# Two chained transformer models on one core: eighteen expert weight tiles instead of sixteen, and another join between the models

## The chip, the cores and the metric

The kernel runs on one core of a Trainium2 chip. Its time is the device time of one execution in microseconds (us). Three executions gave 896.29, 896.9 and 897.87 us, a median of 896.9. Profiles are of single executions.

A core has the engines PE (TensorE, matrix products), DVE (VectorE), ACT (ScalarE) and POOL (GpSimd), each with its own instruction stream, and SP (SyncE), which here issues nearly all loads. They wait for each other by semaphores.

## The reference

Two models run one behind the other on the same 256 tokens of width 1024, all in float32. The first has a latent attention with a convolution branch and then a mixture of 32 experts. The change touches the experts, the norm between the models, and the start of the second.

```python
# first_block, its end: one layer (DEPTH = 1), 256 tokens of width 1024
h = rmsnorm(x, norm2_g[l]) * (1.0 + sc2) + sh2
x = x + gt2 * hierarchical_moe(h, ...)
...
return rmsnorm(x, final_norm_g)

def hierarchical_moe(h, rg_w, rg_b, re_w, re_b, e_gate, e_up, e_down):
    t = h.reshape(-1, D)
    g_prob = jax.nn.softmax((t @ rg_w + rg_b).astype(jnp.float32), axis=-1)
    g_val, g_idx = lax.top_k(g_prob, 1)                     # 1 of 4 groups
    ...
    e_val, e_idx = lax.top_k(jax.nn.softmax(e_sel, axis=-1), TOP_K_IN_GROUP)   # 2 of its 8 experts
    ...
    for gi in range(N_GROUPS):
        a = jnp.einsum('td,edf->tef', t, e_gate[gi])        # f = 128
        u = jnp.einsum('td,edf->tef', t, e_up[gi])
        hid = jax.nn.silu(a) * u * combine[:, gi, :, None]
        out = out + jnp.einsum('tef,efd->td', hid, e_down[gi])
    return out.reshape(B, S, D)

# second_block, layer 0: a gated delta mixer, layer 1: an attention with forget gates
mod = cond @ ada_w[i] + ada_b[i]
shift, scale, gate = jnp.split(mod[:, None, :], 3, axis=-1)
h = rmsnorm_2(x, norm_w[i]) * (1 + scale) + shift
x = x + gate * mixer(h, ...)
```

The norm at the end of the first model and the first norm of the second follow on each other directly.

## The kernel before

**Order of work.** `block1_rest` does attention, convolution and output projection of the first model (to about 280 us). `moe` and `moe_loop` route the tokens and run the experts (to about 402 us). `join` adds the experts' output to the residual and does both norms at once, and `gdn` (to about 716 us) and `fox` are the two layers of the second model. A matrix product in near full precision is split in a high and a low part, and its weights pass from `raw` tiles (as loaded) to `hl` tiles (split). An object `feed` puts weight jobs (load, split, products) between other work.

**Experts.** Each token goes to two of 32 experts, and each expert takes up to 32 tokens into its slots; tokens beyond that go to an overflow tile. The experts are worked off in quads of four: eight quads, and the overflow tile as the fifth of nine rounds. For a round i, `s1` is the products with gate and up weights (`ffn1`, L1321), `turn` a transpose (L1333), `s2` the products with the down weights (`ffn2`, L1347), whose result is scaled by `gt2` (`eys`, L1352) and split in `eyh` and `eyl`, and `s3` adds the rows back to the tokens in PSUM (`ffn3`, L1365 and L1366). `pair` gathers the tokens of two quads by a product with a one-hot matrix `hot` (L1401).

**Weights.** The weights of a quad are six tiles of 1 MB (128 x 2048 floats): four with gate and up of one expert, two with the downs of two experts each, 48 tiles in all. A tile lies in a slot of a list `ECYC`, which is gone through in turn: slots of their own (`ex`), of a small ring (`r`), and `raw` and `hl` slots that the first model no longer needs. Sixteen are asked for before the experts start. From then on `weights(i + 1)` asks for the next quad in round i, so that SP issues a load when the slot's last reader is done. SP issues in order: what stands behind a waiting load waits too. In round 2 SP, like every engine, reads the number of overflow tiles (`tot`), and in round 4 all pass a branch (`spill`, L1832) around further overflow tiles, which is not taken with this data: one tile is enough.

**Counts.** The rank of a token in its expert comes from small products in a PSUM tile (`rk`); the count of each expert (`cnt_`, L1678 and L1679) is written to the same tile, behind a copy by DVE (`rks`, L1676). On PE the order is ranks, counts, gather of the first pair.

**Join.** For each half of the columns and each half of the tokens, x + experts is formed by DVE (L1862), multiplied by the norm weight `gfin` (`xg`, by POOL L1864 and DVE L1867), and both are squared and summed (ACT L1858, for one piece DVE `jx`). Small DVE operations and a power on POOL (L1884) give one factor per token; the rows are scaled (`xn`, ACT L1888, DVE L1889), and PE turns them by 16 transposes with the identity (L684). `feat` then applies the modulation of the second model and splits for the first products (L483). The final norm weight lies in a tile `gfin` of a pool that is made when the experts have ended. `A(4)` and `A(5)` are products that make modulation rows of the second model from `adaA` and `adaX` weights (`ada_mul`, L530).

## Time and profile before

| | |
|---|---|
| median of three executions | 896.9 us |
| the profiled execution | 898.32 us |
| its span, first to last instruction | 896.5 us |
| mean granted clock of TensorE | 0.951 |
| PE busy | 789.2 us (88%) |
| DVE busy | 582.7 us (65%) |
| ACT busy | 395.5 us (44%) |
| POOL busy | 287.4 us (32%) |
| moved by DMA | 190.23 MB, mean 212 GB/s |

The busy shares are means over stages that differ: a stage in which PE waits for loaded weights and one in which PE sets the pace stand in the same sum. The granted clock is given as a share of 2.4 GHz, 0.50 being 1.2 GHz. 1.8 us lie between the span and the time of the profiled execution.

### The profile page before, as it was taken

The numbers are of one execution on the slowest core, as the hardware profiler recorded it, in microseconds if no ns is written. First come the engines' busy times: TensorE is split into PE (matmuls) and PEld (weight loads), VectorE is DVE, ScalarE is ACT, GpSimd is POOL, SyncE is SP. The second block draws the span as 40 slices with busy tenths as digits, with TensorE's granted clock in tenths as the row PEclk, the third lists the DMA queues.
The fourth block names the chain that finished last, engine by engine and source line by source line (L and its number), as shares of the span: only waits on it lengthen the run. The fifth ranks groups of instructions, "written<-read, shape, count | busy, mean of one in ns | idle before, by whom it ended". The sixth has DMA issues, their size and how long they took to land.

```text
span 896.5 us, 16456 instructions
## 1 busy us (share of the span) xinstructions
PE 789.2 (88%) x6567; PEld 684.4 (76%) x6567; DVE 582.7 (65%) x1168; ACT 395.5 (44%) x734; POOL 287.4 (32%) x219
## 2 busy tenths in 40 slices
PE   4889798889996998975999799998999998999986
PEld 1578677678885854534789787888998977999976
DVE  1587875755756754336768989568656458667555
ACT  2355433436444222116575244345543462555452
POOL 0144221213323200004273255133354434445433
PEclk9999999999997899996999899899999999999999
DMA  8886667678989599959354267362247654444201
GB/s 286 282 255 208 201 202 253 226 255 302 369 345 345 215 409 372 409 213 334 113 172 144 92 203 269 96 205 81 92 157 268 216 167 138 136 148 142 95 24 48
DMA packets 125813, 190.23 MB, mean 212 GB/s; under 512 B 11243, under 2 KB 84185, under 8 KB 125733
## 3 DMA queue, kind: packets, MB, share of 16 engines
q1 hardware_dynamic: 123252, 185.78, 60.0%
q10 hardware_dynamic: 1984, 1.79, 0.6%
q0 software_dynamic: 496, 1.59, 0.5%
q8 instruction: 52, 0.85, 0.4%
q14 instruction: 29, 0.23, 0.1%
HBM read 187.91 MB, written 1.22 MB: 211 GB/s over the span
## 4 chain that ended last, share of the span: by engine, by line
PE 31%; DVE 13%; POOL 2%; ACT 2%; issue 2%; DMA 0%; POOLq 0%; ACTq 0%; DVEq 0%
PE mm L351 4%; PE mm L352 4%; PE mm L353 4%; DVE cacc L2023 2%; PE mm L483 2%; PE mm L485 2%; PE mm L484 2%; PE tp L2430 1%; DVE zb L2396 1%; PE tp L2437 1%; DVE NU L2229 1%; PE tp L2038 1%; PE mm L391 1%; PE mm L393 1%; PE mm L392 1%
## 5 line engine op out<-in xcount | busy, mean ns | idle before, releaser
L313 POOL TENSOR_TENSOR hl<-raw,hl 128x1024 fp32r<-128x1024 f32 (+3 forms) x82 | 192.5, 2349 | 327.1 <-ACT hl L309 298.7
L309 ACT ACTIVATE hl<-raw 128x1024 fp32r<-128x1024 f32 (+4 forms) x156 | 153.8, 1018 | 45.1 <-DMA raw<-in_w_in_dram 27.7
L313 DVE TENSOR_TENSOR hl<-raw,hl 128x1024 fp32r<-128x1024 f32 (+2 forms) x74 | 98.6, 1333 | 69.5 <-ACT hl L309 69.4
L483 PE MATMUL mm<-h_hi,hl 128*128 128x256 f32 x448 | 135.6, 303 | 3.2 <-DVE b L589 2.5
L485 PE MATMUL mm<-h_hi,hl 128*128 128x256 f32 x448 | 129.9, 290 | 7.0 <-POOL hl L313 3.5
L484 PE MATMUL mm<-h_lo,hl 128*128 128x256 f32 x448 | 129.3, 289 | 0.7 <-DVE h_lo L699 0.7
L483 PEld LDWEIGHTS mm<-h_hi,hl 128*128 128x128 f32 x448 | 88.0, 196 | 10.0 <-ACT hl L309 4.0
L485 PEld LDWEIGHTS mm<-h_hi,hl 128*128 128x128 f32 x448 | 87.8, 196 | 8.8 <-POOL hl L313 4.8
L484 PEld LDWEIGHTS mm<-h_lo,hl 128*128 128x128 f32 x448 | 88.1, 197 | 1.0 <-DVE h_lo L699 1.0
L351 PE MATMUL mm<-hl,h4h 128*128 128x256 f32 (+1 forms) x256 | 75.9, 296 | 1.1 <-ACT h4h L696 0.7
L352 PE MATMUL mm<-hl,h4h 128*128 128x256 f32 (+1 forms) x256 | 72.2, 282 | 0.9 <-DVE hl L313 0.5
L353 PE MATMUL mm<-hl,h4l 128*128 128x256 f32 (+1 forms) x256 | 72.4, 283 | 0.4 <-DVE h4l L699 0.2
L1046 DVE SCALAR_TENSOR_TENSOR tp<-uq,convw,tp 128x256 f32<-128x256 f32 x120 | 58.4, 487 | 3.1
L351 PEld LDWEIGHTS mm<-hl,h4h 128*128 128x128 f32 x256 | 48.8, 190 | 2.7 <-ACT h4h L696 0.9
L352 PEld LDWEIGHTS mm<-hl,h4h 128*128 128x128 f32 x256 | 48.7, 190 | 1.3 <-DVE hl L313 0.7
L353 PEld LDWEIGHTS mm<-hl,h4l 128*128 128x128 f32 x256 | 48.5, 190 | 1.0 <-DVE h4l L699 1.0
L1321 PE MATMUL tp<-ew,xs 128*32 128x256 f32 x528 | 42.7, 401 | 6.4 <-DMA ew<-in_expert_w_up_dram 6.4
L2023 DVE SCALAR_TENSOR_TENSOR cacc<-mm,aconv,cacc 128x255 f32<-128x255 f32 (+2 forms) x96 | 38.8, 472 | 13.6 <-ACT cacc L2020 13.6
L1321 PEld LDWEIGHTS tp<-ew,xs 128*32 128x32 f32 x528 | 26.7, 115 | 23.4 <-issue 14.6
L351 PE MATMUL mm<-hl,h_hi 128*128 128x256 f32 x128 | 38.4, 300 | 0.0
L352 PE MATMUL mm<-hl,h_hi 128*128 128x256 f32 x128 | 36.4, 284 | 0.0
L353 PE MATMUL mm<-hl,h_lo 128*128 128x256 f32 x128 | 36.2, 282 | 0.0
(684 smaller groups left out, 2007.0 us busy)
## 6 DMA issues: line engine op xcount, KB each, us to landing
raw<-in_ada_w_dram SPq DMA_DIRECT2D x30, 1024.0 KB
raw<-in_a_w_in_dram SPq DMA_DIRECT2D x24, 1024.0 KB
ew<-in_expert_w_gate_dram SPq DMA_DIRECT2D x32, 512.0 KB
ew<-in_expert_w_up_dram SPq DMA_DIRECT2D x32, 512.0 KB
ew<-in_expert_w_down_dram SPq DMA_DIRECT2D x16, 1024.0 KB
raw<-in_b_w_in_dram SPq DMA_DIRECT2D x15, 1024.0 KB
raw<-in_w_in_dram SPq DMA_DIRECT2D x12, 1024.0 KB
raw<-in_a_w_out_dram SPq DMA_DIRECT2D x8, 1024.0 KB
```

The costliest lines, as they stand in the source:

```text
L309: nc.scalar.activation(pc[2][:, ks], v[:, ks], AF.Copy)
L313: eng.tensor_tensor(pc[3][:, ks], v[:, ks], pc[2][:, ks].bitcast(F), OP.subtract)
L351: nc.tensor.matmul(pts[t], a, whi[:, k, :], start=kk == 0, stop=False)
L352: nc.tensor.matmul(pts[t], a, wlo[:, k, :], start=False, stop=False)
L353: nc.tensor.matmul(pts[t], b, whi[:, k, :], start=False, stop=kk == ko - 1)
L391: nc.tensor.matmul(pts[t], a, whi[:, k, :], start=kk == 0, stop=False)
L483: nc.tensor.matmul(p[:, b, :], wa, hh[:, kk, :], start=kk == 0, stop=False)
L484: nc.tensor.matmul(p[:, b, :], wa, hl[:, kk, :], start=False, stop=False)
L485: nc.tensor.matmul(p[:, b, :], wb, hh[:, kk, :], start=False, stop=kk == ko - 1)
L1046: nc.vector.scalar_tensor_tensor(dst, u[:, b, tp:tp + 256], w(b, tp), dst, op0=OP.mult, op1=OP.add)
L1321: nc.tensor.matmul(pg[32 * s:32 * s + 32, :], xs[:, k, c0 + 32 * s:c0 + 32 * s + 32], gu[s][:, :, k * 128:(k + 1) * 128], start=k == 0, st ...
L2023: nc.vector.scalar_tensor_tensor(acc[:, b, sh:], p[:, b, 0:256 - sh], w(b, 3 - sh), acc[:, b, sh:], op0=OP.mult, op1=OP.add)
```

## The change

It has five parts.

1. `ECYC` has eighteen slots: `r4` and `ex4` are new. Expert 0's gate and up go to `r4` already in `block1_rest`, in front of a load of `in_w_in` weights; the other seventeen are asked for in the order `EFIRST`.
2. `ahead` asks for quads 3 to 7 at fixed places: quad 3 after `s2(0)`, quads 4 and 5 in rounds 2 and 3, quads 6 and 7 after rounds 4 and 5. The downs of the last quad are loaded by halves of the columns, all four experts in one tile, so that each half of `ffn2` needs one tile.
3. The counts are emitted with the ranks, ahead of all DVE reads of that tile.
4. In the join, `gfin` lies in slot `r4`. DVE does all adds and multiplies, ACT all eight squares (scaled by 1/32 before the square, so that the sums are means). Instead of scaling the rows and transposing them, PE multiplies by a diagonal `dg` that holds the factors. `mid` puts the `adaA` products, until now later among the `feed` jobs, between the experts and that.
5. Some buffers share tags (`eys` with `part`, `ptj` with `rowp`, `pw`, `pwt`, `PTx`, `xsx`), the buffers of the overflow tile are taken later, and the scratch for GpSimd's DMAs is 4096 bytes.

```diff
-    ECYC = ["ex2", "ex3", "ex1", "r0", "r1", "raw", "ex0", "raw", "raw", "raw", "hl", "hl", "hl", "hl", "r2", "r3"]
+    ECYC = ["r4", "r0", "r1", "raw", "raw", "raw", "raw", "hl", "ex2", "ex3", "ex4", "ex0",
+            "ex1", "hl", "hl", "hl", "r2", "r3"]
+    EFIRST = [8, 9, 10, 1, 2, 11, 12, 3, 4, 5, 6, 7, 13, 14, 15, 16, 17]
...
+        self.e0 = self.ring(4, "ew", F, 2, 1024)
+        for i, n in enumerate(("gate", "up")):
+            nc.sync.dma_start(self.e0[:, i, :], inp["expert_w_" + n].rearrange("l g e (p j) f -> (l g e) p (j f)", j=8)[0])
...
+                elif q == 7:
+                    nc.sync.dma_start(by_columns(e), down[28:32, :, 512 * (s - 4):512 * (s - 4) + 512]
+                                      .rearrange("e f d -> f e d"))
...
+                for t in range(2):
+                    nc.tensor.matmul(cnt_, self.onesb, mm[:, t], start=t == 0, stop=t == 1)
                 self.picks(hot, iom, rk, 0)
...
                 nc.vector.tensor_copy(rks, rk)
                 rk = rks
-                nc.tensor.matmul(cnt_, self.onesb, mm[:, 0], start=True, stop=False)
-                nc.tensor.matmul(cnt_, self.onesb, mm[:, 1], start=False, stop=True)
...
             if 0 < i < 8:
                 weights(i + 1)
+            if i in (2, 3):
+                ahead(i + 2)
...
             s2(i)
+
+            if i in (0, 4, 5):
+                ahead({0: 3, 4: 6, 5: 7}[i])
...
+                nc.vector.tensor_add(x[:, t, sl], acc[t][n], x[:, t, sl])
+                nc.vector.tensor_mul(xg[:, t, sl], x[:, t, sl], gf[:, sl])
+                for a, o in enumerate((x, xg)):
+                    nc.scalar.activation(junk[:, a, sl], o[:, t, sl], AF.Square, scale=D ** -0.5,
+                                         accum_out=ss[:, a, n, t:t + 1])
+        mid()
...
+        dg = U("dg", "dg", 2, 128)
+        for t in range(2):
+            nc.vector.tensor_scalar(dg[:, t], self.ident, r[:, 1, t:t + 1], None, op0=OP.mult)
...
-        xn = U("xn", "P1", 2, 1024)
         for n in range(2):
             sl = slice(512 * n, 512 * n + 512)
-            nc.scalar.activation(xn[:, 0, sl], xg[:, 0, sl], AF.Copy, scale=r[:, 1, 0:1])
-            nc.vector.tensor_scalar(xn[:, 1, sl], xg[:, 1, sl], r[:, 1, 1:2], None, op0=OP.mult)
...
+                if dg is None:
+                    self.nc.tensor.transpose(o, src, self.ident)
+                else:
+                    self.nc.tensor.matmul(o, src, dg[:, t], start=True, stop=True)
...
-        gf = U("gfin", "MM", 2048)
+        gf = self.ring(4, "gfin", F, 2048)
...
-        feed.add(gq[0], A(4, "A0", "A1"), gq[1], A(5, "X0", "X1"), *gq[2:])
+        fill = A(4, "A0", "A1")
+        feed.add(gq[0])
+        fill.todo = fill.load()
+        feed.add(gq[1], A(5, "X0", "X1"), *gq[2:])
+        def mid():
+            feed.q.insert(0, fill)
+            feed.finish(fill)
```

On SP around the branch (`spill`; in the rows L1832 before, L1859 after), before the change: quad 4's last up and its downs, the branch, then the first loads of quad 5.

```order
L1517 DMA ew<-in_expert_w_up_dram 128x1024
L1520 DMA ew<-in_expert_w_down_dram 128x2x1024 x2
L1832 COMPARE_AND_BRANCH x15
L1832 UNCONDITIONAL_BRANCH x16
L1516 DMA ew<-in_expert_w_gate_dram 128x1024
```

The same place after the change, quad 4's downs, the whole of quad 5, the branch, and the first load of quad 6.

```order
L1535 DMA ew<-in_expert_w_down_dram 128x2x1024 x2
L1528 DMA ew<-in_expert_w_gate_dram 128x1024
L1529 DMA ew<-in_expert_w_up_dram 128x1024
L1528 DMA ew<-in_expert_w_gate_dram 128x1024
L1529 DMA ew<-in_expert_w_up_dram 128x1024
L1528 DMA ew<-in_expert_w_gate_dram 128x1024
L1529 DMA ew<-in_expert_w_up_dram 128x1024
L1528 DMA ew<-in_expert_w_gate_dram 128x1024
L1529 DMA ew<-in_expert_w_up_dram 128x1024
L1535 DMA ew<-in_expert_w_down_dram 128x2x1024 x2
L1859 COMPARE_AND_BRANCH x15
```

Quad 5's ten loads moved ahead of the branch.

On PE at the join, before: the last rows of `ffn3`, then the transposes and the first products of the second model.

```order
L1365 MATMUL tp<-eyh,PTs 128x512
L1366 MATMUL tp<-eyl,PTs 128x512
L684 MATMUL tp<-ident,xn 128x128 x16
L483 MATMUL mm<-h_hi,hl 128x256
L484 MATMUL mm<-h_lo,hl 128x256
```

After the change (one row of the program is one matmul; a plain float32 one leaves two records in a trace):

```order
L1376 MATMUL tp<-eyh,PTs 128x512
L1377 MATMUL tp<-eyl,PTs 128x512
L530 MATMUL tp<-adaA_5870,crep_153 32x512 x4
L530 MATMUL tp<-adaA_5871,crep_153 32x512 x4
L689 MATMUL tp<-dg,xg 128x128 x16
L483 MATMUL mm<-h_hi,hl 128x256
```

The `adaA` products moved in front of the turns, and the turns are products with `dg`.

On DVE at the join, before, from the last `eys` on:

```order
L1352 TENSOR_TENSOR eys<-tp,gt2r 128x512
L1862 TENSOR_TENSOR x<-mm,x 128x512 x2
L1354 TENSOR_TENSOR eyl<-eys,eyh 128x512
L1862 TENSOR_TENSOR x<-tp,x 128x512 x2
L1867 TENSOR_TENSOR xg<-x,gfin 128x512 x2
L1873 TENSOR_TENSOR jx<-x 128x512
L1874 TENSOR_REDUCE jss<-jx 128x1
```

After, from the same `eys` to the diagonal:

```order
L1363 TENSOR_TENSOR eys<-tp,gt2r 128x512
L1886 TENSOR_TENSOR x<-mm,x 128x512
L1365 TENSOR_TENSOR eyl<-eys,eyh 128x512
L1887 TENSOR_TENSOR xg<-x,gfin 128x512
L1886 TENSOR_TENSOR x<-mm,x 128x512
L1887 TENSOR_TENSOR xg<-x,gfin 128x512
L1886 TENSOR_TENSOR x<-tp,x 128x512
L1887 TENSOR_TENSOR xg<-x,gfin 128x512
L1886 TENSOR_TENSOR x<-tp,x 128x512
L1887 TENSOR_TENSOR xg<-x,gfin 128x512
L1895 SCALAR_TENSOR_TENSOR jr<-jss 128x2
```

One add stands before the last `eyl` instead of two, and the multiplies stand directly behind their adds.

## Rows read from the trace of the kernel before

**Rows 1.** windows, the experts at full flow (five engines busy, PEclk, DMA share, GB/s)

```profile
314.00:336.00 22.00, 21.64 (x218) 12.03 (x217) 11.28 (x24) 4.80 (x10) 0.00 (x0) 1.00 1.03 409
```

**Rows 2.** windows, columns as in rows 1, seven stretches

```profile
128.00:132.00 4.00, 4.00 (x31) 3.15 (x33) 1.19 (x2) 2.28 (x3) 0.00 (x0) 1.00 0.95 345
340.00:344.00 4.00, 2.67 (x23) 2.47 (x21) 2.68 (x5) 2.12 (x4) 0.00 (x0) 1.00 0.91 344
344.00:348.00 4.00, 3.34 (x42) 1.57 (x43) 1.42 (x3) 0.63 (x1) 0.00 (x0) 1.00 0.86 292
348.00:352.00 4.00, 4.00 (x42) 2.31 (x34) 1.93 (x4) 0.91 (x2) 0.00 (x0) 1.00 0.96 372
392.00:396.00 4.00, 4.00 (x24) 2.10 (x25) 0.64 (x3) 0.28 (x1) 0.00 (x0) 1.00 0.08 26
404.00:426.00 22.00, 11.51 (x68) 11.22 (x68) 15.67 (x22) 14.42 (x27) 9.53 (x6) 0.61 0.97 335
412.00:416.00 4.00, 2.17 (x10) 2.18 (x11) 2.36 (x6) 3.26 (x6) 2.27 (x3) 0.50 1.09 359
```

**Rows 3.** waits of SP, 230 to 412 us (us, times, longest)

```profile
SPq L2112 <- DVE eyl L1354: 18.8, 1, 18.8
SPq L1520 <- PE tp L1321: 14.0, 1, 14.0
SPq L1516 <- PEq L1832: 9.1, 1, 9.1
```

**Rows 4.** waits of PE, 285 to 416 us

```profile
PE tp L1321 <- DMA ew<-in_expert_w_up_dram: 6.4, 4, 2.0
```

**Rows 5.** timeline (start, length), DVE and PE around the counts

```profile
287.98 2.48 DVE L1647 SCALAR_TENSOR_TENSOR xnl<-xs,rstd,xnh 128x1024 fp32r<-128x1024 f32 x2
...
291.99 0.19 PE L1678 MATMUL tp<-mm,onesb 128*128 128x32 bf16 x1 [4.65 <-DVE rks L1676]
...
298.04 7.40 PE L1321 MATMUL tp<-ew,xs 128*32 128x256 f32 x128
```

**Rows 6.** timeline, the join

```profile
400.04 0.68 DVE L1354 TENSOR_TENSOR eyl<-eys,eyh 128x512 fp32r<-128x512 f32 x1
...
401.31 1.29 DVE L1862 TENSOR_TENSOR x<-tp,x 128x512 f32<-128x512 f32 x2 [0.59 <-PE tp L1366]
401.35 0.39 PE L1366 MATMUL tp<-eyl,PTs 128*128 128x512 f32 x1
...
405.81 2.36 DVE L1867 TENSOR_TENSOR xg<-x,gfin 128x512 f32<-128x512 f32 x2 [3.21 <-DMA gfin<-in_final_norm_g_dram]
...
410.69 0.63 ACT L1858 ACTIVATE gfin<-xg 128x512 bf16<-128x512 f32 x1
411.23 0.19 ACT L1858 ACTIVATION_READ_ACCUMULATOR gfin<-xg 128x1 f32 x1
...
412.28 0.73 POOL L1884 TENSOR_TENSOR jr<-jr,pexp 128x2 f32<-128x2 f32 x1 [3.00 <-DVE jr L1883]
...
413.83 3.67 PE L684 MATMUL tp<-ident,xn 128*128 128x128 f32 x16 [12.09 <-ACT xn L1888]
```

**Rows 7.** timeline, PE, the first half of the last quad

```profile
383.34 8.71 PE L1321 MATMUL tp<-ew,xs 128*32 128x256 f32 x62 [2.01 <-DMA ew<-in_expert_w_up_dram]
```

**Rows 8.** PE groups by shape, 426 to 716 us (busy, mean ns | idle before)

```profile
L2430 PE MATMUL tp<-wk,At 128*128 128x128 f32 x64 | 8.4, 275 | 0.0
...
L2038 PE MATMUL tp<-ident,G 128*128 128x128 f32 x32 | 4.6, 276 | 1.0 <-DVE G L2167 1.0
...
L530 PE MATMUL tp<-adaA,crep 128*32 128x512 f32 x16 | 3.4, 990 | 0.0
...
L530 PE MATMUL tp<-adaX,crep 128*32 128x512 f32 x16 | 1.9, 598 | 0.0
```

**Rows 9.** timeline, SP and ACT where expert 0's tile is to be loaded

```profile
124.94 10.16 SPq L520 DMA_DIRECT2D raw<-in_ada_w_dram  x2
...
129.72 1.06 ACT L309 ACTIVATE hl<-raw 128x1024 fp32r<-128x1024 f32 x1 [2.83 <-DMA raw<-in_w_in_dram]
```

More of the change, by code (lines that the diff above doesn't have):

```diff
@@ L1350, in ffn2 @@
             yl = self.sm.tile([128, 512], R, name="eyl", tag="hft", bufs=2)
-            ys = pool.tile([128, 512], F, name="eys", bufs=1)[:M]
+            ys = self.sm.tile([128, 512], F, name="eys", tag="part", bufs=1)[:M]
             nc.vector.tensor_mul(ys, py[:M], self.gt2[:M, sl])
@@ L1392, in slot_side @@
             nc.tensor.transpose(p[:m, t * 128:(t + 1) * 128], pw[:, t, c0:c0 + m], self.ident)
-        jk = pool.tile([128, 256], B16, name="ptj", bufs=1)
+        jk = self.sm.tile([128, 256], B16, name="ptj", tag="rowp", bufs=1)
         nc.scalar.activation(jk[:m], p[:m], AF.Copy, accum_out=wslot[:m])
@@ L1547, in moe @@
                 own("eyh", 512, dt=R, bufs=2)
-                own("eys", 512)
+                own("xs8", 8, 32)
+                OH = T("OH", 2, 2, 32)
+                T("e2", 2, 32)
                 for t in ("ex0", "ex1", "ex2", "ex3"):
@@ L1837, in tiles @@
                 wsx = pool.tile([128, 1], F, name="wsx", bufs=1)
[L1838 to L1839 removed]
+                PTx = self.const.tile([128, 256], R, name="PTx", tag="crep1", bufs=1)
+                xsx = pool.tile([128, 8, 32], F, name="xsx", tag="xs8", bufs=1)
                 self.slot_side(pool, pwx, 0, 32, PTx, wsx)
@@ L1866, in join @@
-        for t, sl, n in order[2:]:
-            nc.vector.tensor_mul(xg[:, t, sl], x[:, t, sl], gf[:, sl])
-        for a, i in ((1, 0), (0, 2), (1, 1), (1, 2), (1, 3)):
-            square(a, *order[i])
-        t, sl, n = order[3]
-        sq = self.sm.tile([128, 512], F, name="jx", tag="hft", bufs=2)
-        nc.vector.tensor_mul(sq, x[:, t, sl], x[:, t, sl])
-        nc.vector.reduce_sum(ss[:, 0, t, n:n + 1], sq, axis=AX.X)
-        todo = self.feed.q[0].todo
-        todo.pop(0)()
-        sq = self.sm.tile([128, 2, 2], F, name="jsq", bufs=1)
@@ new lines, in join @@
+        mid()
+        todo = self.feed.q[0].todo
+        r = self.sm.tile([128, 2, 2], F, name="jr", bufs=1)
+        nc.vector.scalar_tensor_tensor(r[:, 0], ss[:, 0, 0], EPS, ss[:, 0, 1], op0=OP.add, op1=OP.add)
+        nc.vector.scalar_tensor_tensor(r[:, 1], r[:, 0], EPS, ss[:, 1, 0], op0=OP.mult, op1=OP.add)
+        nc.vector.tensor_add(r[:, 1], r[:, 1], ss[:, 1, 1])
+        nc.gpsimd.tensor_tensor(r[:, 1], r[:, 1], self.pexp.to_broadcast([128, 2]), OP.pow)
+        dg = U("dg", "dg", 2, 128)
@@ L2730, in build @@
             acc = kern.moe(x)
-        if stop == "1":
-            with tc.tile_pool(name="pj", bufs=1) as pool:
-                kern.join(lambda n, tag, *sh, dt=F: pool.tile([128] + list(sh), dt, name=n, tag=tag, bufs=1), acc, x)
         if stop not in ("1a", "1"):
```

90 lines of the change are left out of this document (39 added, 51 removed).

## The prediction

> **What bounds the kernel now.** I read the page's busy shares first (the table above): TensorE (PE) is busy 88% of the span, so time is to be had where PE stands idle or runs at half clock. The windows name the place: the experts and the join behind them, 290 to 415 us. Three views of that stretch carry the argument.
>
> The windows show the weight stream. At full flow the queues move 409 GB/s [rows 1]. The stream has a dent at the spill branch (344, 292, 372 GB/s in three windows from 340 us) and has ended when 392 us are reached (26 GB/s) [rows 2]. SP, which issues all loads in order, waited 14.0 us for the first expert matmuls to give back a slot, 9.1 us for PE's sequencer at the branch, and 18.8 us for the last `eyl` of the experts before it could load the join's norm weight [rows 3]. Meanwhile the consumer waits for bytes: 6.4 us in four waits of `ffn1` for up weights [rows 4]. So from 304 to 392 us the stream is the bound and PE is close behind it; what counts is when the stream restarts and how much is still to come.
>
> The PE rows before that show the second place: 4.65 us idle in front of the counts, because their PSUM tile is first read by DVE (`rks`) [rows 5]. The third is the join: the last expert matmul starts at 401.35 us, the first transpose at 413.83 after 12.09 us of idle PE; in that gap DVE waited 3.21 us for the norm weight, then came squares, a power, a scaling pass, transposes [rows 6].
>
> **Counts.** PE order stays; only the wait goes. The gather could start behind `hot`, but it reads `xnl` too, two DVE instructions that end at 287.98 + 2.48 = 290.46 us [rows 5]. Start 290.5 at once, against 292.1 now (behind the two counts at 291.99): at least -1.6; the whole idle stretch, -4.65, is the other bound, less the run at half clock. The xs copies that follow had waited for `obase`, a DVE chain behind the counts, and the first of those waits goes too. I take -2.8 for the start of `s1(0)` (298.04 now), bounds -1.6 and -3.8. Nothing is behind it on PE that could lose.
>
> **Tiles and `ahead`.** Before, 16 of 48 tiles are loaded when the experts start; after, 18 (one of them, expert 0's, at 124 us). A tile is 1.05 MB, so two fewer are 2.1 MB / 0.409 = 5.1 us of stream. The restart hangs on `s1(0)`, so it moves by its -2.8. Quad 5 is asked before the branch: the dent is (65 + 117 + 37) GB/s x 4 us = 0.88 MB, 2.1 us. The last downs by column halves let the first half of `ffn2` go with one tile, but their pieces are half as long; the nearest row, 335 GB/s in 404 to 426 us where loads of such pieces run [rows 2], gives 2.1 / 0.335 - 5.1 = 1.1 us, of which half lies ahead of the first half. Against it stands one tile fewer to wait for, of which PE could use less than 1 us. I put the pair at 0. Sum for the landing: -5.1 - 2.8 - 2.1 = -10.0.
>
> PE has to follow. Without its waits it gains 6.4 + 2.8 = 9.2, and the last quad's `ffn1`, which took 8.71 us for 62 records against 7.40 for 128 in the first two [rows 5, 7], gives another 1 to 2. So PE could end 10 to 11 us sooner, just enough: both bounds meet, and the last expert matmul moves by **-10.0** (bounds -7, if a slot's reader or the half clock holds one of them, and -11). PE's own wait at the branch, for DVE's sequencer, stays.
>
> **Join.** `gfin` now loads behind the last downs, so DVE's 3.21 us go. DVE then runs add and multiply in turn; POOL's multiplies, `jx` and its reduce are gone. The last `eyl` stands behind one add (0.64), not two: its `eyh` is there half an add earlier, so **-0.3**. From the end E of the last expert matmul: `eyl` ended 1.0 us before E (400.72 to 401.74); behind it stand a multiply, an add, a multiply, to E + 0.95, then the four of the second half, 0.65 each (from the pair of adds of 1.29 us), to E + 3.6. The last square and its read (0.63, 0.19) end at E + 4.5; ACT's eight squares in a row, each behind its DVE row, end there too. Three small DVE instructions follow (four stand now between 411.42 and 412.28, 0.22 each): E + 5.2. The power, 0.73: E + 5.9; two diagonals of 128 columns, the first matmul at E + 6.4 [rows 6]. So 12.09 becomes 6.4: **-5.7**, bounds -4 (DVE multiplies as slow as the pair of 2.36 us now) and -6.5.
>
> **The turning matmuls.** A transpose by `ident` and a plain f32 matmul by `dg` are not the same. In the trace the plain ones leave two records each: 64 records of 128x128 (32 matmuls) take 8.4 us, 0.26 us per matmul; 32 transposes take 4.6 us, 0.14 each [rows 8]. Here the clock is 0.50 [rows 2] and 16 transposes took 3.67 us, 0.23 each [rows 6]. Sixteen matmuls thus take 4.2 us at full clock, 7.4 to 7.7 at half. PE's first GEMM comes right behind, so the loss is on the path: +4 if the clock stays low as long as now, less as PE does more work in that stretch and the clock may rise sooner, and -0.9 at full clock with the GEMM behind it at full clock too. I take **+1.5**, bounds -0.9 and +4.
>
> The Trainium skill, TensorE: Matmul & The Clock Gate, section Terms, calls transpose mode four times as fast for FP32. By the rows here it is 1.8 times. By the page's factor the sixteen would cost 11 us more at half clock instead of 4.
>
> **adaA moved.** Its 16 records cost 3.4 us in a stretch that PE bounds, at half clock by their 990 ns against 598 of `adaX`, whose 16 take 1.9 [rows 8]. They now stand between the experts and the turns. Its loads stand behind `gfin` (0.5 MB) and one `raw` (1 MB), 3.7 MB with its own 2: at 335 GB/s these land 11 us after the last downs, at 392 - 10 + 11 = 393. E moves from 401.35 + 0.39 to 391.4 and the turns from 413.83 to 397.8, so 3.4 us from 393 on fit in the gap with some 1.4 us to spare. Its `part` copy on ACT stands behind the squares. Gain: **-2.4**, bounds -1.9 (the half clock then hits the GEMM) and -3.4. If the landing is 3 us late the cover is gone and each further us counts in full.
>
> **e0.** 1 MB more in front of `raw<-in_w_in` at 124 us: 2.6 us at 0.409, plus two issues of half a microsecond on SP. ACT waits 2.83 us for that load at 129.72 [rows 9]; it will wait longer. PE was busy throughout, all of 128 to 132 us among it [rows 2], and SP itself stood 10 us in the next issue [rows 9], so the stream has slack right behind. **+0.5**, bounds 0 and +3.5.
>
> The renamed buffers and the smaller scratch cost nothing: `eys` and `ptj` share tags with tiles that are idle during the experts; if `part` were needed there, one ACT copy would wait less than 1 us.
>
> **Sum:** -10.0 - 0.3 - 5.7 + 1.5 - 2.4 + 0.5 = -16.4. The profiled execution took 898.32 us, so 881.9; it is 1.4 above the median 896.9, which becomes **880.5**.
>
> **Rivals.**
>
> *PE or DVE takes over as the bound in the experts* (chance 0.15). With the waits gone PE has little left; if the restart gains nothing because `s1(0)` runs at half clock, or a DVE chain (overflow lists before `ehid`) holds the first turn, the last matmul moves by 7 and the half clock in the turns costs 4: 885 to 886. For it: clock 0.50 around the join and PE busy nearly all of 314 to 336 us [rows 1, 2]. Against: each of the four PE waits names the DMA [rows 4].
>
> *The stream stays where it is* (0.10): the change does not do what it says; tiles 18 on wait for slots, or the rate is 380 instead of 409 (30 tiles, 31.5 MB: +6 us). Then only the dent, the join and `adaA` are left: -10.0 + 6 and the rest -6.4, 886.5.
>
> *All covers hold and the clock rises early* (0.12): -11 - 0.3 - 6.5 - 0.9 - 3.4, 875.
>
> *Transposes four times cheaper than matmuls* (0.03): +11 instead of +1.5 gives 890. The records speak against it. It is the mechanism of the page named above.
>
> *Slower: the overflow tile lands late* (0.03). Its buffers are now taken after quad 3 and cleared only when `ffn2(0)` has read one of them; its gathers then share the queues with quads 3 and 4. `s1(8)` needs it at about 330 us. It is issued near 307; if it landed after 330, each us would hold PE, and PE is what everything waits for. From 16.4 us late on, 347 us, the kernel is slower than before. Against: a tile and a half is 4 us of stream, and the slack is over 20.
>
> **How the numbers follow.** My case, -13 to -20, has 0.56: 877 to 884. Range 872 to 888: it takes in the good case, the first two rivals and the bounds of turns and e0, and leaves out 0.15. A measurement tells 0.2%, 1.8 us, from no change. Faster: all but the last case and a remainder in which several bounds fall together, 0.95; same 0.02; slower 0.03.
>
> **What the profile after would show.** PE's wait for `rks` gone and the gather at 290 to 291; `s1(0)` near 295; no dent at the branch; last up weight landing near 380; the four DMA waits of `ffn1` below 3 us in sum; last expert matmul near 391; no wait for `gfin`; first matmul by `dg` at 397 with 32 records in 4 to 7.7 us; `adaA` before it; the first GEMM at 402 to 404. It would be wrong if the matmuls by `dg` hold PE past 405, if `adaA` starts after 394, or if PE in the experts shows new waits for DVE.

## The result, and the profile after

The changed kernel took 881.39 us (median of four executions, 880.5 to 885.71), the kernel before 896.6 us on the same chip. The means, over six executions of the changed kernel and four of the kernel before, have a ratio of 0.9847, interval 0.9815 to 0.9879, so 13.7 us less (10.8 to 16.6); the medians differ by 15.2 us. 880.5 us was forecast, with a range of 872 to 888. Single executions of one kernel differ by up to 11 us here and their granted clocks by about 0.02, so steps of 2 or 3 us are read from stages, not from totals. The execution in the trace after is the slowest of the four, 885.71 us:

```profile
span 883.8 us, 16485 instructions
...
PE 781.9 (88%) x6583; PEld 677.2 (77%) x6583; DVE 580.1 (66%) x1167; ACT 394.7 (45%) x734; POOL 284.1 (32%) x217
```

The share of PE is what it was, so the page does not tell where the time went. Stages do. The table is worked out from starts of PE rows in the timelines: the start of the output projection of the first model (L351, L353), the first `ffn1`, the end of the last `ffn3`, the first turn or transpose at the join, the first small product of the second model (`wba`, L2134 before, L2154 after), the first transpose of `G`, the last PE row. "After again" is a second trace of the same kernel.

| us | to projection | to first `ffn1` | experts | gap at the join | turns to `wba` | `wba` to `G` | rest |
|---|---|---|---|---|---|---|---|
| before | 247.2 | 50.8 | 103.7 | 12.1 | 11.9 | 18.3 | 445.5 |
| after | 249.4 | 46.6 | 96.8 | 5.8 | 10.4 | 18.2 | 449.5 |
| after again | 250.1 | 45.3 | 95.2 | 5.8 | 10.4 | 17.6 | 449.4 |
| forecast, after less before | +0.5 | -2.8 | -7.2 | -6.0 | +1.5 | -2.4 | 0 |
| after less before | +2.2 | -4.2 | -6.9 | -6.3 | -1.5 | -0.1 | +4.0 |
| after again less before | +2.9 | -5.5 | -8.5 | -6.3 | -1.5 | -0.7 | +3.9 |

The rest holds no edit. It took 444.1 to 449.5 us over all kernels below, which have the same code there, and the granted clock in it goes the other way: 0.98 where it took 444.1 us (quad5_late), 0.97 in before, 0.96 in both traces of after. So its +4 goes with the clock and is not bound to the code; why both traces of this kernel lie at the long end is not known.

**Counts** (timeline after, PE and DVE; compare [rows 5]):

```profile
287.96 0.19 PE L1663 MATMUL tp<-mm,n 128*128 128x32 bf16 x1
...
288.10 0.20 PE L1668 MATMUL tp<-mm,onesb 128*128 128x32 bf16 x2
288.94 2.47 DVE L1671 SCALAR_TENSOR_TENSOR xnl<-xs,rstd,xnh 128x1024 fp32r<-128x1024 f32 x2
...
289.18 1.19 PE L1412 MATMUL tp<-hot,xnh 128*128 128x256 f32 x8 [0.87 <-ACT part L533]
...
291.47 1.86 PE L1412 MATMUL tp<-hot,xnl 128*128 128x256 f32 x7 [0.81 <-DVE xnl L1671]
...
295.98 7.28 PE L1332 MATMUL tp<-ew,xs 128*32 128x256 f32 x128
```

The first row of the ranks in the kernel before:

```profile
287.02 0.21 PE L1641 MATMUL tp<-mm,n 128*128 128x32 bf16 x1
```

The counts have no wait in front of them. The gather starts on `xnh` 1.2 us behind the first rank (5.1 before), of which 0.87 are a wait for ACT's `part`, and waits 0.81 us more in its middle, for the `xnl` named in the forecast. From the first rank to the first `ffn1` it is 8.0 us here and 6.7 in the second trace, against 11.0 before, so the counts are worth 3.0 and 4.3 us. The other 1.2 us of that stage's gain lie ahead of the ranks (39.8 us from the projection before, 38.6 in both traces after), where the counts have no part.

**Experts** (three windows after, columns as in [rows 1]; then waits of SP, 230 to 400 us, and of PE, 280 to 410 us: us in all, times, longest):

```profile
340.00:344.00 4.00, 2.06 (x13) 1.32 (x13) 2.14 (x4) 1.13 (x2) 0.00 (x0) 1.00 1.03 410
344.00:348.00 4.00, 4.00 (x66) 2.12 (x65) 2.08 (x4) 1.26 (x2) 0.00 (x0) 1.00 1.02 400
348.00:352.00 4.00, 4.00 (x27) 1.96 (x26) 1.63 (x4) 0.28 (x1) 0.00 (x0) 1.00 1.03 410
```

```profile
SPq L1528 <- PE tp L1332: 11.6, 2, 11.4
```

```profile
PE tp L1332 <- DMA ew<-in_expert_w_up_dram: 4.5, 2, 2.5
...
PE tp L689 <- DVE dg L1901: 1.9, 1, 1.9
...
PE tp L1344 <- DVE ehid L1337: 1.0, 1, 1.0
```

The dent at the branch (344, 292, 372 GB/s in [rows 2]) is gone, and so are SP's waits of 9.1 and 18.8 us in [rows 3]. SP still waits 11.4 us for the first products to give back a slot, and PE still waits for bytes, 4.5 us instead of 6.4 in [rows 4]: the stream is still the bound. The forecast had asked for less than 3 us of such waits.

**Join** (timeline after; compare [rows 6]):

```profile
392.38 0.40 PE L1377 MATMUL tp<-eyl,PTs 128*128 128x512 f32 x1
...
393.00 1.06 PE L530 MATMUL tp<-adaA,crep 128*32 128x512 f32 x8 [0.22 <-DMA adaA<-in_ada_w_dram]
...
395.63 1.07 PE L530 MATMUL tp<-adaA,crep 128*32 128x512 f32 x8 [1.56 <-DMA adaA<-in_ada_w_dram]
...
397.44 0.73 POOL L1898 TENSOR_TENSOR jr<-jr,pexp 128x2 f32<-128x2 f32 x1 [85.89 <-DVE jr L1897]
...
398.20 0.48 DVE L1901 TENSOR_SCALAR dg<-ident,jr 128x128 f32<-128x128 f32 x2 [0.85 <-POOL jr L1898]
...
398.55 3.84 PE L689 MATMUL tp<-dg,xg 128*128 128x128 f32 x32 [1.85 <-DVE dg L1901]
...
402.14 0.36 PE L483 MATMUL mm<-h_hi,hl 128*128 128x256 f32 x1
```

No DVE row waits for `gfin`. The `adaA` products lie in the gap, the second half 1.56 us late but still 1.85 us ahead of the turns; the power comes 5.1 us after the last expert product starts (10.9 before).

**The start** (after, timeline of ACT and a window):

```profile
132.58 1.06 ACT L309 ACTIVATE hl<-raw 128x1024 fp32r<-128x1024 f32 x1 [6.83 <-DMA raw<-in_w_in_dram]
```

```profile
132.00:136.00 4.00, 0.80 (x8) 0.42 (x4) 2.27 (x4) 2.96 (x4) 0.80 (x1) 1.00 0.40 145
```

And the waits of PE, 120 to 160 us:

```profile
PE mm L483 <- DVE gt L589: 2.2, 1, 2.2
PE tp L1276 <- ACT pp L1279: 2.0, 1, 2.0
```

Here something was lost. ACT's wait of 2.83 us in [rows 9] became 6.83, `pp` stands behind it on ACT and PE waits for that; PE was busy 0.80 of four microseconds.

**Behind the join** (timeline after):

```profile
416.82 2.38 POOL L313 TENSOR_TENSOR hl<-raw,hl 128x1024 fp32r<-128x1024 f32 x1 [6.09 <-ACT hl L309]
416.84 2.40 DVE L1926 TENSOR_SCALAR sp<-sp 128x32 f32<-128x32 f32 x1
...
422.65 0.61 PE L2184 MATMUL tp<-g,trile 128*128 128x32 f32 x2 [2.51 <-DVE beta L2170]
...
423.61 3.64 PE L530 MATMUL tp<-adaX,crep 128*32 128x512 f32 x16
```

Where `adaA` had stood, PE now waits 2.51 us for `beta`, and then runs the `adaX` products, which took 1.9 us in [rows 8], at half clock (0.50 granted): 3.64 us.

### The profile page after: what moved, and what is told of

It reads as the page before. It is cut to its first block, busy times and chain, and to the rows that moved or that the text cites. A ratio compares the mean times of both kernels' runs of the same rounds, so it can differ in the third digit from the quotient of the medians.

```text
span 883.8 us, 16485 instructions
## 1 busy us (share of the span) xinstructions
PE 781.9 (88%) x6583; PEld 677.2 (77%) x6583; DVE 580.1 (66%) x1167; ACT 394.7 (45%) x734; POOL 284.1 (32%) x217
## 4 chain that ended last, share of the span: by engine, by line
PE 45%; DVE 24%; DMA 15%; ACT 6%; issue 5%; POOL 3%; SPq 1%; ACTq 0%; POOLq 0%; DVEq 0%
DMA ew<-in_expert_w_up_dram 6%; DMA raw<-in_w_in_dram 6%; PE mm L351 4%; PE mm L353 4%; PE mm L352 4%; PE mm L483 3%; DVE hl L313 3%; PE mm L485 3%; PE mm L484 3%; DVE cacc L2035 2%; DVE tp L1050 2%; POOL hl L313 2%; PE mm L530 2%; ACT hl L309 2%; DMA ew<-in_expert_w_down_dram 1%
## 5 line engine op out<-in xcount | busy, mean ns | idle before, releaser
L483 PE MATMUL mm<-h_hi,hl 128*128 128x256 f32 x448 | 134.4, 300 | 5.5 <-DVE b L589 2.5
L483 PEld LDWEIGHTS mm<-h_hi,hl 128*128 128x128 f32 x448 | 87.5, 195 | 10.9 <-ACT hl L309 4.1
L351 PE MATMUL mm<-hl,h4h 128*128 128x256 f32 (+1 forms) x256 | 76.3, 298 | 1.1 <-ACT h4h L700 0.7
L353 PE MATMUL mm<-hl,h4l 128*128 128x256 f32 (+1 forms) x256 | 72.8, 284 | 0.4 <-DVE h4l L703 0.2
L351 PEld LDWEIGHTS mm<-hl,h4h 128*128 128x128 f32 x256 | 49.1, 192 | 2.8 <-ACT h4h L700 0.9
L353 PEld LDWEIGHTS mm<-hl,h4l 128*128 128x128 f32 x256 | 48.8, 191 | 1.0 <-DVE h4l L703 1.0
L1332 PE MATMUL tp<-ew,xs 128*32 128x256 f32 x528 | 37.7, 379 | 4.5 <-DMA ew<-in_expert_w_up_dram 4.5
L351 PE MATMUL mm<-hl,h_hi 128*128 128x256 f32 x128 | 38.4, 300 | 0.0
L1332 PEld LDWEIGHTS tp<-ew,xs 128*32 128x32 f32 x528 | 23.1, 110 | 20.0 <-issue 9.3
L353 PE MATMUL mm<-hl,h_lo 128*128 128x256 f32 x128 | 36.3, 283 | 0.0
```

The source lines that it names most:

```text
L351: nc.tensor.matmul(pts[t], a, whi[:, k, :], start=kk == 0, stop=False)
L353: nc.tensor.matmul(pts[t], b, whi[:, k, :], start=False, stop=kk == ko - 1)
L483: nc.tensor.matmul(p[:, b, :], wa, hh[:, kk, :], start=kk == 0, stop=False)
L1332: nc.tensor.matmul(pg[32 * s:32 * s + 32, :], xs[:, k, c0 + 32 * s:c0 + 32 * s + 32], gu[s][:, :, k * 128:(k + 1) * 128], start=k == 0, st ...
```

## The experiments

Each kernel is the changed one with the edit shown, timed beside the kernel before on one chip per group (medians 896.64, 897.03 and 895.53 us in three groups). Stages are in the order of the table above.

### Group 1: one part undone at a time

**e0_stream.** Expert 0's gate and up are asked for with the other tiles, no longer in the attention.

```diff
         self.e0 = self.ring(4, "ew", F, 2, 1024)
-        for i, n in enumerate(("gate", "up")):
-            nc.sync.dma_start(self.e0[:, i, :], inp["expert_w_" + n]...[0])
...
+                nc.sync.dma_start(self.e0[:, 0, :], gate[0])
+                nc.sync.dma_start(self.e0[:, 1, :], up[0])
                 for k, i in enumerate(self.EFIRST):
```

> Expert 0's tile is no longer loaded in the attention stage but as the first of the other seventeen, some 115 us later. Theory: that early load cost 2.4 us in the trace after (PE's shift against before went from -1.3 to +1.1 us across 130 to 255 us, with +4 in between), and the stream before the experts has room for one tile more, so the first gather comes 2 us sooner and the whole kernel takes 879 us, and the shift across the attention stage stays at -1. Rival: what the attention stage lost would have been lost anyway, or the extra 2.6 us of stream delay the restart of the loads: 881 to 883 us.

878.66 us, ratio 0.9818 (0.9785 to 0.985); stages 244.3, 47.4, 95.6, 5.8, 12.6, 18.2, 444.5. ACT's row and PE's window at that place:

```profile
127.81 1.06 ACT L309 ACTIVATE hl<-raw 128x1024 fp32r<-128x1024 f32 x1 [2.82 <-DMA raw<-in_w_in_dram]
```

```profile
132.00:136.00 4.00, 4.00 (x38) 3.45 (x31) 3.83 (x11) 1.30 (x6) 0.80 (x1) 1.00 0.49 142
```

This is the forecast's theory, 879 us. The wait is back at 2.82 us, PE has no hole, and the experts lose nothing by the later load. The totals' intervals overlap; the first stage tells the two apart. It is 248.0 to 250.1 us in the nine traces with the early load (mean 249.2) and 244.3 to 247.5 in the five without, that of before among them (mean 246.4): the early load costs some 2.8 us.

**adaA_late.** The `adaA` products go back among the `feed` jobs.

```diff
-        feed.add(gq[0])
-        fill.todo = fill.load()
-        feed.add(gq[1], A(5, "X0", "X1"), *gq[2:])
+        feed.add(gq[0], fill, gq[1], A(5, "X0", "X1"), *gq[2:])
         def mid():
-            feed.q.insert(0, fill)
-            feed.finish(fill)
+            pass
```

> The adaA products go back behind the first products of the second model; all else as after. Theory: in the gap of the join they keep the granted clock at 1.00. Without them PE is idle for 6 us, the clock in the turns is 0.5 to 0.6, the 32 records of the turns take 7.0 to 7.7 us instead of 3.84, the products behind them start at half clock, and adaA costs 2 to 3.4 us in its old place: 888 to 890 us. Rival: a gap of 6 us leaves the clock up by itself, the turns take 3.9 to 4.2 us and only adaA's own time returns: 883 to 884 us.

881.75 us, 0.9835 (0.9807 to 0.9864), the same as after; stages 249.0, 46.4, 95.9, 5.2, 12.8, 18.3, 447.7. Timeline of PE:

```profile
396.52 6.73 PE L689 MATMUL tp<-dg,xg 128*128 128x128 f32 x32 [5.18 <-DVE dg L1901]
...
412.86 3.60 PE L530 MATMUL tp<-adaA,crep 128*32 128x512 f32 x16
...
424.66 1.92 PE L530 MATMUL tp<-adaX,crep 128*32 128x512 f32 x16
```

Neither number of the forecast came, and moving `adaA` shows no gain. PE spends 3.60 us on `adaA` where the changed kernel waits for `beta` and runs `adaX`; there is no `beta` wait here, and `adaX` comes later, at full clock. With PE idle 5.18 us at the join the turns ran at half clock; but in e0_stream, where `adaA` stood in the gap, they took 6.57 us, and in counts_late 5.33. Over the ten traces that turn with `dg` and have `adaA` in the gap they took 3.84 us three times and 5.29 to 6.57 us seven times. So `adaA` in the gap does not hold the clock up in every run, which was a reason to make this run; whether it helps in the mean is open, as there is only this one run without it.

**turns_ident.** Rows scaled by ACT and DVE, transposed by the identity, as before.

```diff
-        dg = U("dg", "dg", 2, 128)
-        for t in range(2):
-            nc.vector.tensor_scalar(dg[:, t], self.ident, r[:, 1, t:t + 1], None, op0=OP.mult)
+        xn = U("xn", "P1", 2, 1024)
+        for n in range(2):
+            sl = slice(512 * n, 512 * n + 512)
+            nc.scalar.activation(xn[:, 0, sl], xg[:, 0, sl], AF.Copy, scale=r[:, 1, 0:1])
+            nc.vector.tensor_scalar(xn[:, 1, sl], xg[:, 1, sl], r[:, 1, 1:2], None, op0=OP.mult)
...
-        return xg, dg, resid
+        return xn, None, resid
```

> The rows are scaled (ACT and DVE, two instructions each) and turned by transposes with the identity as before; the rest of the new join stays. Theory: at full clock sixteen transposes take 2.0 to 2.6 us instead of 3.84, which pays for the 1.0 to 1.3 us of the scaling pass: 881 us, plus or minus 0.7, and the diagonal itself brought nothing. Rival 1: the scaling pass is what the join gained from, 883 us. Rival 2: plain float32 products cost four transposes, the transposes take 1 us, and the kernel takes 879 us.

879.56 us, 0.9809 (0.9781 to 0.9838); stages 249.4, 47.5, 95.8, 6.5, 11.9, 16.6, 447.2. Timeline of PE, and a window:

```profile
399.07 3.67 PE L687 MATMUL tp<-ident,xn 128*128 128x128 f32 x16 [2.64 <-ACT xn L1902]
...
404.22 0.41 PE L483 MATMUL mm<-h_hi,hl 128*128 128x256 f32 x1
```

```profile
404.00:408.00 4.00, 4.00 (x23) 4.00 (x23) 2.51 (x6) 3.49 (x5) 0.00 (x0) 0.58 0.22 74
```

Gap and turns together are 18.4 us here, 16.2 in both traces of after and 18.0 and 18.4 in adaA_late and e0_stream: no difference beyond their spread, and none in the total. The total is that of rival 2, but not for its reason: the transposes did not take 1 us. The sixteen transposes, 3.67 us, are cheaper than the products with `dg` where those ran mostly at half clock (6.57 and 6.73 us, granted 0.56 and 0.54), but the first GEMM behind them (L483) ran at half clock to about 407 us (0.41 us a product, window 0.58), while behind the products with `dg` it ran at full clock at once. The Trainium skill, TensorE: Matmul & The Clock Gate, Part 4: PE-mode transpose, says that the full clock is not engaged by transpose mode. The sixteen transposes agree with that, at a granted 0.50 here and a mean of 0.53 in the last kernel below; among other products at full clock they keep it (0.14 us each in [rows 8], granted 1.00). On the products behind them that page says nothing, and there the two traces differ.

**counts_late.** The counts go back behind DVE's copy.

```diff
-                for t in range(2):
-                    nc.tensor.matmul(cnt_, self.onesb, mm[:, t], start=t == 0, stop=t == 1)
                 self.picks(hot, iom, rk, 0)
...
                 rk = rks
+                for t in range(2):
+                    nc.tensor.matmul(cnt_, self.onesb, mm[:, t], start=t == 0, stop=t == 1)
```

> The two count products stand behind DVE's copy again; the rest as after. Theory: the first expert products start 2.8 to 3.2 us later (299 instead of 296 us), the stream restarts as much later, and as the stream bounds the experts the whole kernel takes 884 us. Rival: PE or a DVE chain bounds the first rounds anyway, the start moves but the last expert product by less than 1 us: 881 to 882 us.

888.4 us, 0.9904 (0.9875 to 0.9934), which only touches after's interval (to 0.9879); stages 248.9, 50.0, 96.1, 5.1, 11.7, 18.2, 449.5. Waits of PE, 270 to 310 us:

```profile
PE tp L1701 <- DVE rks L1698: 4.7, 1, 4.7
```

The 4.65 us of [rows 5] are back, as 4.7. From the first rank to the first `ffn1` it is 11.5 us, 3.5 and 4.8 more than in the two traces of after, and the experts keep their length, as the theory has it. But the total lies 4.4 us above the 884 of the forecast and 7.0 above after's median, more than the stage explains; where the difference comes from is open.

### Group 2: the tiles, and a repeat

**after_again** is the changed kernel once more.

> The changed kernel itself, unchanged, on the chip of the next three, for a second profile and more times. Theory: the join, the experts and the counts stand as in its first profile (last expert product near 392 us, turns near 398.5), but the clock in the turns is not set by the adaA products: the turns take between 3.8 and 7 us, and what the first profile lost behind 500 us (some 4 us in all) is the granted clock of that execution and is partly gone: median 879 to 882 us. Rival: the losses behind 500 us belong to the change and stand at the same places again, with a profile near 885 us.

883.49 us (879.76 to 887.74), 0.9853 (0.9827 to 0.9879); its stages are in the table. The theory's 879 to 882 us did not come: the rest took 449.4 us again, as the rival says, though kernels with the same code there took down to 444.1.

**sixteen.** Tiles 16 and 17 are asked for with the later quads.

```diff
-    EFIRST = [8, 9, 10, 1, 2, 11, 12, 3, 4, 5, 6, 7, 13, 14, 15, 16, 17]
+    EFIRST = [8, 9, 10, 1, 2, 11, 12, 3, 4, 5, 6, 7, 13, 14, 15]
...
             if i in (0, 4, 5):
+                ahead(2)
                 ahead({0: 3, 4: 6, 5: 7}[i])
```

> The last two of the eighteen tiles (quad 2's downs) are asked for only when the first expert products have run, so that 32 tiles are still to come instead of 30; all else as after. Theory: the stream bounds the experts, so the last up weight lands 5.1 us later, and so does the last expert product (397 instead of 392): 886 us. Rival: PE bounds the experts, since it has little idle time left, and the last product moves by less than 2 us: 881 to 883 us.

883.7 us, 0.9852 (0.982 to 0.9885); stages 249.8, 47.1, 95.2, 5.8, 12.1, 18.2, 446.7. A miss as a test. The row of SP for these two tiles, here, and in the trace after:

```profile
288.80 1.76 SPq L1535 DMA_DIRECT2D ew<-in_expert_w_down_dram  x2
```

```profile
286.49 1.91 SPq L1535 DMA_DIRECT2D ew<-in_expert_w_down_dram  x2
```

SP has nothing else in between, so the two loads go out at the same place of the program, ahead of the first `ffn1`, in whichever list they stand. The run is one more repeat of after.

**quad5_late.** Quad 5 is asked for behind the branch again.

```diff
-            if i in (2, 3):
-                ahead(i + 2)
+            if i == 2:
+                ahead(4)
...
             if i in (0, 4, 5):
+                if i == 4:
+                    ahead(5)
                 ahead({0: 3, 4: 6, 5: 7}[i])
```

> Quad 5 is asked for behind the branch again; all else as after. Theory: SP waits at the branch for PE, the stream has a dent of 2 us there (below 350 GB/s in the 4 us behind the branch), and the end of the experts moves by 2 us: 883.5 us. Rival: eighteen slots leave enough loads in the queue across the branch, no dent, 881 us.

880.58 us, 0.9828 (0.9804 to 0.9852); stages 248.7, 45.4, 95.2, 5.8, 11.7, 18.2, 444.1. Window:

```profile
340.00:344.00 4.00, 2.64 (x29) 1.07 (x32) 1.51 (x4) 0.64 (x2) 0.00 (x0) 1.00 1.03 406
```

No dent and nothing lost, as the rival says, so the place where quad 5 is asked for is not what removed the dent.

**e0_adaX.** e0_stream's edit, and `adaX` one job earlier:

```diff
-        feed.add(gq[1], A(5, "X0", "X1"), *gq[2:])
+        feed.add(A(5, "X0", "X1"), *gq[1:])
```

> Expert 0's tile in the stream of the other seventeen (as in the run before), and the adaX products ahead of the second group of the next products, so that they come some 10 us earlier on PE. Theory: in after PE waits 2.5 us for the softplus chain on DVE (beta) and then runs adaX at half clock, 3.64 us instead of 1.9; with adaX ahead of that wait PE has work while the chain runs, and both shrink: 3 us less than with expert 0's tile alone, 875.5 us. Rival: the adaX loads (2 MB, 6 us) now stand ahead of the weights of the first products, which come later than PE wants them, and what was gained is lost there: 878 to 881 us.

877.19 us (876.99 to 877.73), 0.9783 (0.9768 to 0.9798): below the interval of after_again in the same group, by 6.3 us in the medians. Of the 5.7 us between the two profiled spans 4.9 lie in the rest, which neither edit touches, so the total does not show what the two are worth. Stages 247.5, 46.5, 96.1, 5.1, 11.7, 16.7, 444.5. Timeline of PE:

```profile
410.53 1.92 PE L530 MATMUL tp<-adaX,crep 128*32 128x512 f32 x16
...
423.63 0.65 PE L2050 MATMUL tp<-ident,G 128*128 128x128 f32 x4 [1.26 <-DVE G L2187]
```

`adaX` runs at full clock directly behind `wba`, PE comes later to the product that had waited for `beta`, and that wait is gone. PE now waits 1.26 us for DVE one step on, at `G`. The stage from `wba` to `G` is 16.7 us instead of 17.6 to 18.2; but it is 16.6 in turns_ident without this edit and 18.9 in best with it, so a gain is not shown.

### Group 3: slots, branch, norm weight, and a combination

**slots16.** Before's sixteen slots and order of asking, no early load, no `ahead`.

```diff
-    ECYC = ["r4", "r0", "r1", "raw", "raw", "raw", "raw", "hl", "ex2", "ex3", "ex4", "ex0",
-            "ex1", "hl", "hl", "hl", "r2", "r3"]
-    EFIRST = [8, 9, 10, 1, 2, 11, 12, 3, 4, 5, 6, 7, 13, 14, 15, 16, 17]
+    ECYC = ["ex2", "ex3", "ex1", "r0", "r1", "raw", "ex0", "raw", "raw", "raw", "hl", "hl", "hl", "hl", "r2", "r3"]
+    EFIRST = list(range(16))
...
-            if i in (2, 3):
-                ahead(i + 2)
...
-            if i in (0, 4, 5):
-                ahead({0: 3, 4: 6, 5: 7}[i])
```

> Sixteen slots in the order of before, no early load of expert 0, quads asked for as before; the slots of the branch's spare tiles, the column halves, counts and join stay as after. From the start of the first expert products to the last one it took 103.3 us before and 94.8 to 96.4 in all kernels with eighteen slots so far. Theory: two tiles more to come after the start are 5.1 us of stream, and the stream is the bound: 100 to 102 us for that stretch, and with expert 0's load gone (2.6 us) 883 to 886 us in all. Rival: the two tiles are no part of the gain, since PE had little idle time left, and the stretch stays at 95 to 97 us: 878 to 880 us.

888.56 us, 0.9928 (0.99 to 0.9956); stages 246.9, 45.3, 104.5, 5.1, 10.6, 18.1, 446.4. Waits of PE (280 to 416 us) and of SP (230 to 416 us), and three windows:

```profile
PE tp L1329 <- DMA ew<-in_expert_w_up_dram: 6.2, 4, 2.0
```

```profile
SPq L1525 <- PE tp L1355: 15.2, 3, 7.8
...
SPq L1532 <- PE tp L1329: 9.9, 1, 9.9
```

```profile
304.00:308.00 4.00, 3.73 (x25) 2.19 (x17) 2.43 (x6) 0.75 (x2) 0.42 (x1) 0.83 0.86 260
308.00:312.00 4.00, 4.00 (x24) 3.47 (x25) 3.46 (x10) 3.41 (x9) 0.00 (x0) 1.00 0.95 314
340.00:344.00 4.00, 2.22 (x10) 0.58 (x11) 1.76 (x4) 0.79 (x2) 0.00 (x0) 0.86 1.02 405
```

The experts take 104.5 us, as before's 103.7, with the 6.2 us in four waits for up weights of [rows 4], and yet the window at the branch has no dent (405 GB/s). The slots with the order and places of asking are thus worth the whole gain of that stage, 8 to 9 us. But this stream has a hole elsewhere: 260 and 314 GB/s from 304 to 312 us, where after has 404 and 414 and where SP stands for `ffn2` (L1355) to give back slots. Against 409 GB/s that is 0.98 MB, or 2.4 us, about what the dent was before (0.88 MB, 2.1 us). With 5.1 us for two more tiles it makes 7.5 of the 8.8 us by which this stage is longer than the mean of the eleven other traces with eighteen slots and no dent (95.7 us, 95.2 to 96.8). So the run does not say that a dent costs nothing, and tiles and order were not tried apart.

**spare_early.** quad5_late's edit, and the branch's two spare tiles take the slots that quad 5's third and fourth tile come to.

```diff
-                    extra.extend(ering(t) for t in ("r1", "raw"))
+                    extra.extend(ering(t) for t in ("r2", "r3"))
```

> As after, but the spare tiles of the branch lie in slots that quad 5 needs, and quad 5 is asked for behind the branch (quad 5 asked for behind the branch alone had changed nothing). Theory: what made the dent before was that the next load's slot was one of the branch's spare tiles and could be given back only when PE had passed the branch; with that wait the dent comes back (SP waits over 8 us for PE's sequencer, a window of 4 us below 350 GB/s), and the last expert product comes 2 to 8 us later: 884 to 889 us. Rival: with eighteen slots the loads in flight cover it, no dent, 880 to 883 us.

884.65 us, 0.9884 (0.9858 to 0.991); stages 249.4, 46.5, 97.5, 5.8, 12.0, 18.2, 446.3. A wait of SP, 230 to 400 us, and a window:

```profile
SPq L1528 <- PEq L1861: 10.4, 1, 10.4
```

```profile
340.00:344.00 4.00, 2.06 (x16) 1.21 (x18) 2.00 (x4) 1.13 (x2) 0.00 (x0) 1.00 0.68 211
```

This makes the dent again: SP waits 10.4 us for PE's sequencer at the branch, as 9.1 us in [rows 3], and the window falls to 211 GB/s. The load stands behind the branch because its slot belongs to a tile that the branch may read. So it was in the kernel before: there the spare tiles lie in `ex2` and `ex3`, the slots to which the first two tiles of quad 5 come. The changed kernel has them in `r1` and `raw`, to which none of quad 5 comes; the list of changes does not name this. The missing bytes, (406 - 211) GB/s x 4 us = 0.78 MB, would be 1.9 us of stream, and the stage is 97.5 us, 1.8 above the mean of the eleven (95.7; 95.2 in quad5_late, 96.8 in after), as the theory has it.

**gfin_late.** The norm weight in its own tile, as before.

```diff
-        gf = self.ring(4, "gfin", F, 2048)
+        gf = U("gfin", "MM", 2048)
```

> The final norm weight lies again in a tile of the pool that is made when the experts have ended; the rest of the new join stays, and what stands behind that load on SP (one raw tile, adaA, adaX) waits with it. Theory: the load leaves only at the last eyl, DVE's first multiply waits 3 us for it, adaA lands some 10 us after the end of the experts and PE has its products ahead of the turns: from the last expert product to the turns 12 us instead of 6, 887 to 889 us. Rival: only the load itself counts, 3 us: 884 us.

883.83 us, 0.987 (0.9846 to 0.9895); stages 248.0, 45.5, 95.3, 6.6, 12.1, 18.2, 449.3. Where SP issued that load, and a wait of SP, 360 to 400 us:

```profile
380.19 0.34 SPq L2124 DMA_DIRECT2D gfin<-in_final_norm_g_dram  x1
```

```profile
SPq L2124 <- PE tp L1332: 5.0, 1, 5.0
```

A miss as well, though the total is the rival's: with the other buffers of the changed kernel this place came free with the last `ffn1`, not with the last `eyl` of [rows 3], so before's wait was not made again. The gap is 0.8 us longer. What the load alone was worth stays open.

**best.** e0_stream, `adaX` one job earlier, and turns_ident together (their diffs stand above).

> Expert 0's tile in the stream of the others, adaX ahead of the next products, and rows scaled and turned by transposes; the rest as after. Theory: the gains of the single runs add up: 2.6 us for expert 0, 3 us for adaX (877.2 us together, measured), and the transposes 0 to 2 us: 875 to 877 us. Rival: the transposes bring nothing or lose the scaling pass of 1.3 us: 877 to 879 us.

879.23 us (873.19 to 881.77), 0.9805 (0.9768 to 0.9842), not shown to beat e0_adaX; stages 245.9, 45.2, 95.4, 6.5, 10.9, 18.9, 446.7. Timeline of PE:

```profile
392.97 3.52 PE L687 MATMUL tp<-ident,xn 128*128 128x128 f32 x16 [2.73 <-ACT xn L1902]
...
397.86 0.28 PE L483 MATMUL mm<-h_hi,hl 128*128 128x256 f32 x1
...
407.89 3.64 PE L530 MATMUL tp<-adaX,crep 128*32 128x512 f32 x16
```

The 875 to 877 us of the forecast did not come. Here the GEMM ran at full clock from its second product on behind the transposes, and `adaX`, behind `wba`, fell into a stretch at half clock. So neither choice of turn fixes the clock behind it.

## Why the prediction was right, and where its terms were not

The sum was -16.4 us and 13.7 were measured. Counts, tiles and join carried it, and their prices held to about 1.5 us. `e0`, `adaA` and the turns were each off by 2 to 3 us, not all to one side, and that they nearly cancel is luck.

- **Counts, -2.8** (bounds -1.6 and -3.8): right in its mechanism, 3.0 and 4.3 us from the ranks to the first `ffn1`, and 3.5 and 4.8 by counts_late. The step "Start 290.5 at once" was too late: the gather reads `xnl` only in its second group, and started on `xnh` at 289.2. Between the two traces the gather's clock differs, its third group takes 1.70 us in one and 1.11 in the other. The stage gained 1.2 us more ahead of the ranks, which was no term of the sum.
- **Tiles and `ahead`, -7.2 behind the first `ffn1`** (-5.1 for two tiles, -2.1 for the dent): the stage gave -6.9 and -8.5, and both prices fit. Putting the dent back cost 1.9 us of stream and 1.8 of the stage (spare_early); with the two tiles out and a hole of 2.4 us it is 8.8 us (slots16). What failed is the step that names the dent's cause, "Quad 5 is asked before the branch". Asked for behind it, nothing is lost (quad5_late); the slots of the branch's spare tiles make the dent. Whether asking ahead would have removed it with the spare tiles left in their old slots was not run. The column halves of the last downs, put at 0, had no run.
- **Join, -6.0**: -6.3, and -5.5 to -7.0 over all the runs that have it. The chain of DVE and ACT rows was laid out rightly: the last multiply ends 3.6 us behind the last expert product, as forecast, and the last square 4.4 for 4.5. No run puts the old join back as a whole, so its 6.3 us is read from the stage and its rows; how much of it is the norm weight's load is not settled.
- **Turns, +1.5** (bounds -0.9 and +4): the stage shrank by 1.5 us in both traces of after, outside the better bound, where the clock was 1.00 in the turns; it grew by 0.7 in e0_stream and 0.9 in adaA_late, where it was 0.56 and 0.54. Over the ten traces with `dg` and `adaA` in the gap it is 11.5 us in the mean, 0.4 less than before. The term rested on a clock that one profile could not give, and that the traces of after drew the good side is luck. The price at half clock, 7.4 to 7.7 us, was too high by a microsecond. No gain or loss against transposes is shown.
- **`adaA` moved, -2.4**: nothing. The step that failed is "3.4 us in a stretch that PE bounds": that stretch is not PE's alone. In after PE reaches the product that waits for `beta` 11.2 us behind the start of `wba`, and DVE's chain ends at 13.6. With 3.4 us of `adaA` PE would come at 14.6, so by estimate only 1 of the 3.4 us is there to be gained, and `adaX`, the next job, then runs at half clock, 1.7 us longer. adaA_late, with `adaA` back in its place, has no wait there and takes the same 18.3 us. In the profile of before the cover showed only as a product that takes 3.4 us, with no wait for `beta` behind it.
- **e0, +0.5** (bounds 0 and +3.5): 2.8, within its bounds and near the upper. The step that failed is "the stream has slack right behind". ACT's wait grew by 4 us, and behind that wait stood rows that PE needed; PE's full window at 128 to 132 us in [rows 2] said nothing of the next one.

The balance of the profiled pair against the sum, by stages: 1.7 lost at the start, 2.3 with `adaA`, 4.0 in the rest and 0.3 in the experts; 1.4 gained up to the first `ffn1`, 3.0 in the turns, 0.3 at the join. -16.4 + 3.6 = -12.8, and the spans have -12.7 (896.5 to 883.8). Two of the signs of being wrong showed faintly: the second half of `adaA` started at 395.6, behind the 394 that was set, but still ahead of the turns, and PE has a new wait of 1.0 us for DVE in the experts, for `ehid`. Of the rivals, none came about: PE's waits in the experts still name the DMA, the stream did move, and transposes are not four times cheaper. In turns_ident they cost 3.67 us at half clock against 6.57 and 6.73 for products, 1.8 times, as in [rows 8].

## What to carry to other kernels

A job that fills an engine on a stretch can be a cover for another engine's chain: before it is moved, look at what that chain would make the engine wait for, and which job moves up into the place. A load that is put ahead of others on an in-order queue costs the consumer of the next load, so look at what that one waits for already, and for how long the work in front of it lasts. Where a branch may read a tile, a load into that tile's slot that stands behind the branch waits until the branch is passed, 9.1 and 10.4 us here, and all loads behind it wait too: give such tiles slots that the next loads do not need.
